# Feed-forward up products of a Strassen-type kernel: a new order of the seven products, with sums formed in PSUM from ScalarE's copies

## The chip, the cores and the metric

The kernel runs on one core of a Trainium2 chip. The metric is the device time of one execution in microseconds. The kernel before has a median of 3085.41 us in three runs (3083.14 to 3085.58).

## What is computed

One layer of a hybrid diffusion backbone on 2048 latent and 128 context tokens of width 1024. The change touches the first half of the feed-forward part alone, here cut from the reference:

```python
def finish_layer(x, ao, co, gate_a, shift_f, scale_f, gate_f, ...):
    mix = jnp.concatenate([ao, co], axis=-1) @ w_out
    x = x + gate_a * rms_norm(mix, g_attn_post)
    u = rms_norm(x, g_ffn_pre) * (1.0 + scale_f) + shift_f
    gu = u @ w_ffn_in                                  # 1024 -> 2 * 2816
    h = jax.nn.silu(gu[..., :D_FF]) * gu[..., D_FF:]
    return x + gate_f * rms_norm(h @ w_ffn_out, g_ffn_post)
```

## The kernel before

The program is written in the order of the work; a scheduling layer then sets the order of instructions on each engine, with a timeline of its own, so neighbours in the code need not be neighbours on an engine. Each engine runs its own list strictly in order. All DMAs are issued from one queue, SP's.

The product u @ w_ffn_in is a 2 by 2 block product by a Strassen-Winograd scheme: seven products in place of eight. The 17 token tiles are cut in three chunks (c = 0, 1, 2) of 320, 384 and 384 columns, and the 2816 hidden columns in 22 slices (f); `up_unit` (L948 on) does one (c, f), so there are 66 units. A unit is seven products of 12 matmuls each (L956, L957, L959), since every operand is split in a high and a low part (`split`, L81 on ScalarE makes the high part, L82 on VectorE the low one) and three of the four part products are taken, over four slices of the contraction.

Weights of a unit: `wi_raw` loads two 512 KB tiles, `wi_ops` (L908 on) makes the seven weight operands from the four blocks a11, a12, a21, a22 with four sums s1 to s4 by GpSimd (L918, tile st, 2 buffers) and seven splits. The operands lie in three buffers of two operands and one of two buffers for the seventh, so a unit's first operands can be written when the unit before is done with its own first two.

Token operands: seven as well. `build_tile` (L829 on) loads a tile of 128 tokens, GpSimd scales its rows (L835), TensorE transposes it in eight pieces (L841), four into one PSUM bank, and each piece is modulated on its way out of PSUM (L842: times one scalar per partition, plus another). `build_pair` takes two such tiles, forms differences (tile td, L859, GpSimd) and hands seven operands to `out`. For chunk 0 this happens ahead of the units, between the matmuls of the output projection (tile psx), and the operands stay on the chip. For chunks 1 and 2 it happens inside the units of the chunk before, one pair after each of f = 2, 8 and 14 (`build_spilled`): each operand is split into tile hl, which has one buffer, and stored (u2d<-hl); the next operand's split waits until that store has landed.

PSUM: eight banks, as four tags a, b, c, d with two buffers each. A unit takes one of each (ba, bb, bc_, bd), the transposes of `build_spilled` take banks of tag d. In a unit before, ScalarE copies the first product out to SBUF (p1, L965), VectorE adds it to the second (L968) and to the fifth (L973), adds the third and subtracts the fourth (L975, L976), and adds the seventh (L983); products 5, 6 and 7 are added by TensorE onto what stands in banks bb, ba and bc_. ScalarE takes the silu of both gates (L979, L984), VectorE and GpSimd multiply (L981, L986). The results (hid) go to memory for the down products (tile psy), which follow all 66 units.

## Time and profile before

| | us |
|---|---|
| median of three runs | 3085.41 |
| the profiled execution, its own time | 3085.89 |
| its span, first to last instruction | 3084.1 |
| first matmul of the up products | 1551.07 |
| first matmul of chunk 1 / chunk 2 / last unit | 1874.41 / 2234.20 / 2540.08 |
| last matmul of the up products | about 2557.3 |
| busy in the span: TensorE / VectorE / ScalarE / GpSimd | 2914.8 / 2082.6 / 1348.7 / 1242.9 |

The profiled execution is 1.8 us longer than its span and 0.5 us longer than the median. A busy TensorE is not TensorE at its peak, since matmuls overlap and their ends are modelled: what a stage loses is read from the spacing of matmul starts. The list of waits names, for each instruction that stood idle before it ran, what released it.

### The profile page before, as it was taken

What the parts mean: (1) busy time and instruction counts of PE and PEld (TensorE: products, weight loads), DVE (VectorE), ACT (ScalarE), POOL (GpSimd) and SP (SyncE); (2) the same over time, 40 slices, a digit from 0 to 9 for tenths busy, and PEclk for the clock granted to TensorE, in tenths of its full rate; (3) what the DMA queues carried; (4) which work ended last, traced back from release to release, by engine and by line L of the source; (5) the groups of instructions that cost most, each with busy time, mean ns of one, the idle gap of its engine ahead of it and who ended that gap; (6) DMA issues with size and microseconds to landing.
All of it is one profiled execution on the core that took longest, in us unless ns stands there. A gap on an engine that the chain in (4) does not pass through costs nothing.

```text
span 3084.1 us, 47310 instructions
## 1 busy us (share of the span) xinstructions
PE 2914.8 (95%) x16921; PEld 2653.6 (86%) x16921; DVE 2082.6 (68%) x4158; ACT 1348.7 (44%) x2383; POOL 1242.9 (40%) x1114
## 2 busy tenths in 40 slices
PE   4899989999999999999999989999999999999998
PEld 3778879998999999988888888999999998788886
DVE  7999568787788887764477775776665554554443
ACT  3323236666565665653344433333333333444432
POOL 7313135554545544532256654554544540111110
PEclk8999999999999999999999999999999999999999
DMA  7777564453454444457645465444632325766663
GB/s 249 249 246 246 171 196 123 136 183 113 136 166 127 139 150 132 119 164 223 183 136 156 150 195 193 145 148 134 238 137 97 102 99 193 239 223 219 219 216 120
DMA packets 351180, 525.25 MB, mean 170 GB/s; under 512 B 33089, under 2 KB 264673, under 8 KB 349153
## 3 DMA queue, kind: packets, MB, share of 16 engines
q1 hardware_dynamic: 350944, 522.23, 52.8%
q8 instruction: 133, 2.18, 0.3%
q14 instruction: 103, 0.84, 0.1%
HBM read 393.79 MB, written 128.34 MB: 169 GB/s over the span
## 4 chain that ended last, share of the span: by engine, by line
PE 65%; DVE 12%; DMA 9%; issue 7%; POOL 4%; ACT 2%; SPq 1%; POOLq 0%; DVEq 0%; ACTq 0%
PE psg L956 6%; PE s L502 6%; PE psg L959 6%; PE psg L957 6%; PE psy L1087 4%; PE psy L1086 4%; PE psy L1085 4%; PE t L546 3%; DVE wi L82 3%; DMA raw<-in_w_fi 2%; PE pq L239 2%; POOL st L918 2%; PE psx L725 2%; PE psx L726 2%; PE psx L724 2%
## 5 line engine op out<-in xcount | busy, mean ns | idle before, releaser
L956 PE MATMUL psg<-u,wi 128*128 128x384 f32 (+1 forms) x1848 | 615.6, 334 | 47.2 <-ACT wi L81 21.1
L957 PE MATMUL psg<-u,wi 128*128 128x384 f32 (+1 forms) x1848 | 606.1, 328 | 0.0
L959 PE MATMUL psg<-u,wi 128*128 128x384 f32 (+1 forms) x1848 | 590.6, 330 | 6.0 <-DVE wi L82 6.0
L505 DVE TENSOR_SCALAR_CACHE_REDUCE e<-s 128x436 f32<-128x436 f32 (+2 forms) x648 | 373.8, 600 | 90.0 <-PE s L502 73.4
L956 PEld LDWEIGHTS psg<-u,wi 128*128 128x128 f32 x1848 | 350.0, 189 | 65.7 <-ACT wi L81 29.6
L502 PE MATMUL s<-km,qt 128*128 128x436 f32 (+1 forms) x1280 | 345.7, 374 | 12.1 <-DVE e L505 9.1
L959 PEld LDWEIGHTS psg<-u,wi 128*128 128x128 f32 x1848 | 347.7, 190 | 10.8 <-DVE wi L82 10.3
L957 PEld LDWEIGHTS psg<-u,wi 128*128 128x128 f32 x1848 | 350.4, 190 | 0.1
L82 DVE TENSOR_TENSOR wo<-rawo,wo 128x1024 fp32r<-128x1024 f32 x132 | 167.0, 1265 | 248.4 <-ACT wo L81 243.7
L82 DVE TENSOR_TENSOR wi<-st,wi 128x512 fp32r<-128x512 f32 x264 | 235.2, 895 | 127.6 <-ACT wi L81 126.1
L510 ACT ACTIVATE e<-e,nm 128x2176 f32<-128x2176 f32 (+1 forms) x136 | 274.0, 2015 | 78.4 <-DVE nm L509 77.7
L81 ACT CAST wi<-st 128x512 fp32r<-128x512 f32 x264 | 163.0, 620 | 323.8 <-POOL st L918 166.2
L1087 PE MATMUL psy<-wo,hhl 128*128 128x512 f32 x748 | 285.8, 391 | 1.8 <-DVE hhl L82 1.8
L1086 PE MATMUL psy<-wo,hhl 128*128 128x512 f32 x748 | 286.3, 390 | 0.9 <-DVE wo L82 0.9
L1085 PE MATMUL psy<-wo,hhl 128*128 128x512 f32 x748 | 285.8, 390 | 0.0
L81 ACT CAST wo<-rawo 128x1024 fp32r<-128x1024 f32 x132 | 139.2, 1054 | 296.2 <-PE psy L1087 286.4
L502 PEld LDWEIGHTS s<-km,qt 128*128 128x128 f32 x1280 | 211.0, 192 | 24.4 <-DVE e L505 15.9
L82 DVE TENSOR_TENSOR atl<-t,ath 128x512 fp32r<-128x512 f32 (+2 forms) x292 | 187.1, 650 | 34.7 <-ACT ath L81 33.9
L81 ACT CAST ath<-t 128x512 fp32r<-128x512 f32 (+2 forms) x292 | 157.2, 554 | 116.2 <-PE t L546 107.6
L918 POOL TENSOR_TENSOR st<-raw,st 128x512 f32<-128x512 f32 x66 | 103.0, 1561 | 231.1 <-DVE wi L82 231.1
L1058 POOL TENSOR_TENSOR rr<-rr,mhalf 128x1 f32<-128x1 f32 x17 | 13.1, 779 | 450.4 <-DVE rr L1057 450.4
L82 DVE TENSOR_TENSOR wi<-raw,wi 128x512 fp32r<-128x512 f32 x198 | 176.6, 892 | 15.7 <-ACT wi L81 15.7
(264 smaller groups left out, 7092.6 us busy)
## 6 DMA issues: line engine op xcount, KB each, us to landing
raw<-in_w_fi SPq DMA_DIRECT2D x132, 512.0 KB, 4.1
rawo<-in_w_fo SPq DMA_DIRECT2D x132, 512.0 KB, 3.4
fu<-ud SPq DMA_DIRECT2D x256, 256.0 KB, 4.7
raw<-in_w_ada SPq DMA_DIRECT2D x48, 512.0 KB, 5.3
u2d<-hl SPq DMA_DIRECT2D x42, 512.0 KB, 3.7
u<-u2d SPq DMA_DIRECT2D x14, 1536.0 KB, 9.4
hr<-hid SPq DMA_DIRECT2D x110, 192.0 KB, 3.5
hid<-hid SPq DMA_DIRECT2D x88, 192.0 KB, 2.1
```

The lines of the kernel that those rows point to most:

```text
L81: S.copy(h, src)
L82: (eng or V).tensor_tensor(l, src, h.bitcast(F32), op=ALU.subtract)
L502: mm = T.matmul(ps[:, :n], qt[:, s, m, t * P:(t + 1) * P], km[m][:, k0:k0 + n], start=(s == 0), stop=(s == 1))
L505: V.tensor_scalar(et[:, k0:k0 + n], ps[:, :n], SCALE, None, op0=ALU.mult, op1=ALU.max, accum_out=mx[:, ci:ci + 1])
L510: S.activation(et[:, :nk], et[:, :nk], AF.Exp, bias=nm, scale=1.0, accum_out=sm[:, t, m:m + 1])
L918: G.tensor_tensor(t, x, y, op=op)
L956: T.matmul(ps[:, :n], h[:, ks], u[:, 0, kt, :n], start=start and kt == 0, stop=False, skip_group_check=not start)
L957: T.matmul(ps[:, :n], h[:, ks], u[:, 1, kt, :n], start=False, stop=False, skip_group_check=not start)
L959: T.matmul(ps[:, :n], l[:, ks], u[:, 0, kt, :n], start=False, stop=stop and kt == 3, skip_group_check=not start)
L1085: T.matmul(banks[i][:, b, :], hh, woh_[:, bs], start=(f == 0), stop=False)
L1086: T.matmul(banks[i][:, b, :], hh, wol_[:, bs], start=False, stop=False)
L1087: T.matmul(banks[i][:, b, :], hl, woh_[:, bs], start=False, stop=(f == NF - 1))
```

## The change

It has four parts.

1. **Another order and other sums.** Product 1 goes to bank ba and ScalarE copies it, PSUM to PSUM, into bb; product 2 goes to bc_ and ScalarE copies it to SBUF (p5); product 3 is added by TensorE onto bb, and ScalarE copies bb into bd; products 4, 5, 6 and 7 are added onto ba, bb, bd and bb again. VectorE adds p5 to bb (c22, ahead of product 7) and to bd (u2), and multiplies the silu of ba with bb itself. Per unit VectorE has three operations outside the splits in place of six, ScalarE three copies in place of one.
2. **The weight operands** are made in the order in which the new products use them: a11, s1, s2, a12, s3, s4, a22 (before a11, s2, s1, a22, s3, a12, s4). The token operands are numbered to match.
3. **Modulation** of the built tiles is ScalarE's (Identity with scale and bias from memory) in place of VectorE's: 40 pieces ahead of the units and 96 inside them.
4. **Banks.** The transposes of `build_spilled` take tag c (before d). In the first two units one matmul of 512 columns is added on each of bb and bd, so that later matmuls there add onto what ScalarE wrote.

```diff
--- before.py
+++ after.py
@@ -839,8 +840,8 @@
             for a in range(4):
                 kt = 4 * kk + a
                 T.transpose(up[:, a, :], row[:, kt * P:(kt + 1) * P], ident)
-                V.tensor_scalar(ur[:, kt, :], up[:, a, :], modc[:, 2, c, kt:kt + 1], modc[:, 3, c, kt:kt + 1],
-                                op0=ALU.mult, op1=ALU.add)
+                S.activation(ur[:, kt, :], up[:, a, :], AF.Identity, scale=modc[:, 2, c, kt:kt + 1],
+                             bias=modc[:, 3, c, kt:kt + 1])
         return ur
 
     def build_pair(pair, bank, out):
@@ -860,13 +861,13 @@
             return t
 
         out(0, w, b11)
-        out(5, w, b21)
-        out(6, w, b22)
+        out(3, w, b21)
+        out(5, w, b22)
         t = diff(b12, b11)
-        out(2, w, t)
+        out(1, w, t)
         t2_ = diff(b22, t)
-        out(1, w, t2_)
-        out(3, w, diff(t2_, b21))
+        out(2, w, t2_)
+        out(6, w, diff(b21, t2_))
         out(4, w, diff(b22, b12))
 
     def pst_bank():
@@ -928,15 +929,15 @@
                 dst.append((q[:, 0], q[:, 1]))
         split(*dst[0], a11)
         s1 = total(a21, a22, ALU.add)
+        split(*dst[1], s1)
         s2 = total(s1, a11, ALU.subtract)
-        split(*dst[1], s2)
-        split(*dst[2], s1)
-        split(*dst[3], a22)
-        s4 = total(a12, s2, ALU.subtract)
+        split(*dst[2], s2)
+        split(*dst[3], a12)
         s3 = total(a11, a21, ALU.subtract)
         split(*dst[4], s3)
-        split(*dst[5], a12)
-        split(*dst[6], s4)
+        s4 = total(a12, s2, ALU.subtract)
+        split(*dst[5], s4)
+        split(*dst[6], a22)
         return dst
 
     def t(tag, n, bufs=1):
@@ -948,42 +949,43 @@
     def up_unit(c, f, ws, us):
         n = widths[c]
 
-        def product(ps, i, start, stop):
+        def product(ps, i, start):
             h, l = ws[i]
             u = us[i]
             for kt in range(4):
                 ks = slice(kt * P, (kt + 1) * P)
-                T.matmul(ps[:, :n], h[:, ks], u[:, 0, kt, :n], start=start and kt == 0, stop=False, skip_group_check=not start)
-                T.matmul(ps[:, :n], h[:, ks], u[:, 1, kt, :n], start=False, stop=False,
-                         skip_group_check=not start)
-                T.matmul(ps[:, :n], l[:, ks], u[:, 0, kt, :n], start=False, stop=stop and kt == 3,
-                         skip_group_check=not start)
+                T.matmul(ps, h[:, ks], u[:, 0, kt, :n], start=start and kt == 0, stop=False, skip_group_check=not start)
+                T.matmul(ps, h[:, ks], u[:, 1, kt, :n], start=False, stop=False, skip_group_check=not start)
+                T.matmul(ps, l[:, ks], u[:, 0, kt, :n], start=False, stop=kt == 3, skip_group_check=not start)
 
         ba, bb, bc_, bd = (bank(x) for x in "abcd")
-        product(ba, 0, True, True)
-        p1_ = t("p1", n)
-        S.copy(p1_, ba[:, :n])
-        product(bb, 1, True, True)
+        if c == 0 and f < 2:
+
+            for x in (bb, bd):
+                T.matmul(x, ws[0][0][:, :P], ws[0][0], start=True, stop=True)
+        ba, bb, bc_, bd = (x[:, :n] for x in (ba, bb, bc_, bd))
+        product(ba, 0, True)
+        S.copy(bb, ba)
+        product(bc_, 1, True)
+        p5 = t("p5", n)
+        S.copy(p5, bc_)
+        product(bb, 2, False)
+        S.copy(bd, bb)
+        product(ba, 3, False)
+        sg = t("sg", n)
+        S.activation(sg, ba, AF.Silu)
+        product(bb, 4, False)
+        c22 = t("c22", n)
+        V.tensor_tensor(c22, bb, p5, op=ALU.add)
+        product(bd, 5, False)
         u2_ = t("u2", n)
-        V.tensor_tensor(u2_, bb[:, :n], p1_, op=ALU.add)
-        product(bc_, 2, True, True)
-        product(bd, 3, True, True)
-        product(bb, 4, False, True)
-        u3 = t("u3", n)
-        V.tensor_tensor(u3, bb[:, :n], p1_, op=ALU.add)
-        c22 = t("c22", n)
-        V.tensor_tensor(c22, bc_[:, :n], u3, op=ALU.add)
-        V.tensor_tensor(u3, u3, bd[:, :n], op=ALU.subtract)
-        product(ba, 5, False, True)
-        sg = t("sg", n)
-        S.activation(sg, ba[:, :n], AF.Silu)
-        ha = t("hid", n, 2)
-        V.tensor_tensor(ha, sg, u3, op=ALU.mult)
-        product(bc_, 6, False, True)
-        V.tensor_tensor(u2_, u2_, bc_[:, :n], op=ALU.add)
+        V.tensor_tensor(u2_, bd, p5, op=ALU.add)
         S.activation(u2_, u2_, AF.Silu)
         hb = t("hid", n, 2)
         G.tensor_tensor(hb, u2_, c22, op=ALU.mult)
+        product(bb, 6, False)
+        ha = t("hid", n, 2)
+        V.tensor_tensor(ha, sg, bb, op=ALU.mult)
         if c:
             dma(hidd[c][f][:, 0:n], ha)
             dma(hidd[c][f][:, n:2 * n], hb)
@@ -1001,7 +1003,7 @@
             split(hl[:, 0, :, :w], hl[:, 1, :, :w], src)
             dma(u2d[c, i][:, :, :, k * P:k * P + w], hl[:, :, :, :w])
 
-        build_pair(chunks[c][k], lambda: bank("d"), out)
+        build_pair(chunks[c][k], lambda: bank("c"), out)
 
     def u_load(pool_, i, c):
         u = pool_.tile([P, 2, 4, 384], F32R, tag="u", name="u2", bufs=2 if pool_ is pua else 7)
```

What this does to the order on ScalarE in the steady part, one unit of chunk 2 (wi are weight operands, st the sums, psg the PSUM banks). Before:

```order
L81 CAST wi_26337<-raw4_26226 128x512
L81 CAST wi_26337<-st_26345 128x512
L965 COPY p1_26246<-psg_26230 128x384
L81 CAST wi_26338<-st_26343 128x512
L81 CAST wi_26338<-raw4_26228 128x512
L81 CAST wi_26340<-st_26353 128x512
L984 ACTIVATE u2_26123<-u2_26123 128x384
L979 ACTIVATE sg_26315<-psg_26230 128x384
L81 CAST wi_26339<-st_26355 128x512
L81 CAST wi_26339<-raw4_26226 128x512
```

Now:

```order
L81 CAST wi_26101<-raw4_25991 128x512
L971 COPY p5_26022<-psg_25995 128x384
L81 CAST wi_26098<-raw4_25989 128x512
L81 CAST wi_26098<-st_26104 128x512
L973 COPY psg_25996<-psg_25994 128x384
L976 ACTIVATE sg_26049<-psg_25993 128x384
L81 CAST wi_26099<-st_26108 128x512
L81 CAST wi_26099<-raw4_25989 128x512
L81 CAST wi_26100<-st_26114 128x512
L968 COPY psg_26129<-psg_26128 128x384
L983 ACTIVATE u2_26077<-u2_26077 128x384
L81 CAST wi_26100<-st_26118 128x512
```

The two silus and seven casts are still there; L965's copy has become L968, L973 and L971, and L968, the copy of a unit's first product, stands between the two casts of its third weight buffer.

ScalarE again, in the first build (after f = 2 of chunk 0), at the last two operands that are stored from hl. Before:

```order
L81 CAST hl_18859<-td_18857 128x512
L81 CAST wi_19288<-st_19304 128x512
L81 CAST wi_19288<-raw4_19173 128x512
L81 CAST wi_19425<-raw4_19312 128x512
L965 COPY p1_19332<-psg_19316 128x320
L81 CAST wi_19425<-st_19433 128x512
L81 CAST wi_19426<-st_19431 128x512
L81 CAST wi_19426<-raw4_19314 128x512
L81 CAST hl_18865<-td_18863 128x512
L984 ACTIVATE u2_19207<-u2_19207 128x320
```

Now:

```order
L81 CAST hl_18857<-td_18855 128x512
L976 ACTIVATE sg_19227<-psg_19171 128x320
L81 CAST wi_19279<-st_19288 128x512
L81 CAST wi_19279<-raw4_19167 128x512
L81 CAST wi_19280<-st_19294 128x512
L81 CAST hl_18863<-td_18861 128x512
L968 COPY psg_19309<-psg_19308 128x320
L983 ACTIVATE u2_19255<-u2_19255 128x320
```

The casts into hl stand among the weight casts as before, but a PSUM copy (L968) now stands right behind one. Over all six builds, between a cast into hl of a difference (td) and the cast into hl ahead of it, ScalarE's list had 105 instructions in 24 stretches before, and has 132 now; in 9 of the 24 places a copy L968 or L973 stands among the next three instructions.

TensorE at the transposes of the second tile in that build. Before (banks psg_18802 and psg_18815 take the transposes):

```order
L959 MATMUL psg_19038<-u0_0_16972,wi_19008 128x320
L841 MATMUL psg_18802<-ident_60,row_18789 128x128
L841 MATMUL psg_18815<-ident_60,row_18811 128x128
L956 MATMUL psg_18900<-u0_4_16976,wi_18871 128x320
L957 MATMUL psg_18900<-u0_4_16976,wi_18871 128x320
L959 MATMUL psg_18900<-u0_4_16976,wi_18871 128x320
L956 MATMUL psg_18900<-u0_4_16976,wi_18871 128x320
L957 MATMUL psg_18900<-u0_4_16976,wi_18871 128x320
```

Now (banks psg_18813 and psg_18822):

```order
L957 MATMUL psg_19034<-u0_3_16975,wi_19005 128x320
L958 MATMUL psg_19034<-u0_3_16975,wi_19005 128x320
L842 MATMUL psg_18813<-ident_60,row_18809 128x128
L959 MATMUL psg_19034<-u0_3_16975,wi_19005 128x320
L957 MATMUL psg_19034<-u0_3_16975,wi_19005 128x320
L842 MATMUL psg_18822<-ident_60,row_18809 128x128
L958 MATMUL psg_19034<-u0_3_16975,wi_19005 128x320
L959 MATMUL psg_19034<-u0_3_16975,wi_19005 128x320
L842 MATMUL psg_18813<-ident_60,row_18809 128x128
L842 MATMUL psg_18822<-ident_60,row_18809 128x128
L957 MATMUL psg_19035<-u0_4_16976,wi_19006 128x320
L958 MATMUL psg_19035<-u0_4_16976,wi_19006 128x320
```

Ten matmuls or more stood between two transposes into one bank before (three times in the six builds only two); now the two banks of a tile are filled side by side, most of the rounds stand 20 or more matmuls apart, and ten rounds in the six builds stand two to five matmuls apart.

## Rows read from the trace of the kernel before

**Rows 1.** Busy time by stretch: the last stretch of the output projection with the building of chunk 0's operands, chunk 0, chunk 1, 21 units of chunk 2, the last unit. Columns: length, then busy time and instructions of TensorE, its weight loads, VectorE, ScalarE and GpSimd, granted clock, share of DMA, GB/s.

```profile
1399.00:1551.00 152.00, 152.00 (x686) 124.15 (x684) 67.33 (x115) 58.37 (x131) 34.97 (x43) 1.00 0.64 197
1551.07:1874.41 323.34, 293.64 (x1896) 281.05 (x1897) 251.54 (x359) 132.45 (x250) 192.73 (x134) 0.98 0.50 154
1874.41:2234.20 359.79, 338.01 (x1898) 328.00 (x1897) 239.33 (x358) 132.47 (x244) 181.30 (x128) 0.99 0.52 175
2234.20:2540.08 305.88, 305.88 (x1766) 305.72 (x1765) 175.78 (x273) 112.30 (x210) 151.50 (x105) 1.00 0.33 111
2540.08:2557.30 17.22, 14.94 (x85) 14.30 (x85) 10.00 (x15) 5.69 (x8) 1.00 (x1) 1.00 0.36 116
```

**Rows 2.** The timeline of TensorE in chunk 0, at two matmuls that stand eight steps apart in a dense stretch (start, length).

```profile
1859.96 0.31 PE L956 MATMUL psg<-u,wi 128*128 128x320 f32 x1
...
1861.13 0.31 PE L959 MATMUL psg<-u,wi 128*128 128x320 f32 x1
```

**Rows 3.** Waits of TensorE's weight loads in chunks 0 and 1 (1551 to 2235 us): who waited for whom, us in total, times, longest.

```profile
PEld psg L956 <- ACT wi L81: 29.4, 27, 4.0
PEld psg L956 <- DVE u L968: 11.0, 13, 2.6
PEld psg L959 <- DVE wi L82: 10.3, 16, 1.2
PEld psg L956 <- DVE c L975: 5.4, 4, 3.2
PEld psg L956 <- DVE u L976: 4.8, 6, 0.8
PEld psg L956 <- DMA u<-u2d: 3.7, 1, 3.7
PEld psg L956 <- issue: 3.4, 2, 2.1
PEld psg L956 <- ACT p L965: 1.9, 3, 0.9
PEld psg L956 <- DVE ur L842: 1.4, 3, 0.6
PEld psg L841 <- DVE ur L842: 0.7, 1, 0.7
```

**Rows 4.** The same in chunk 2 (2235 to 2558 us).

```profile
PEld psg L956 <- DVE c L975: 1.6, 1, 1.6
PEld psg L956 <- DVE u L968: 1.4, 1, 1.4
```

**Rows 5.** Busy time by stretch, columns as in Rows 1: two of the six stretches of 3.4 us in chunks 0 and 1 in which the granted clock was half.

```profile
1737.80:1741.20 3.40, 3.40 (x15) 3.40 (x14) 3.40 (x6) 1.49 (x4) 1.33 (x1) 0.50 0.55 158
2079.10:2082.50 3.40, 3.25 (x11) 3.16 (x11) 3.37 (x8) 1.68 (x4) 0.00 (x0) 0.51 0.55 160
```

**Rows 6.** VectorE's groups in the up products (busy us, mean ns of one, idle before and what ended it).

```profile
L842 DVE TENSOR_SCALAR ur<-psg,modc 128x128 f32<-128x128 f32 x96 | 36.8, 402 | 14.5 <-PE psg L841 14.4
L981 DVE TENSOR_TENSOR hid<-sg,u 128x384 f32<-128x384 f32 x44 | 32.0, 727 | 5.0 <-ACT sg L979 3.9
L975 DVE TENSOR_TENSOR c<-psg,u 128x384 f32<-128x384 f32 x44 | 24.4, 555 | 1.2
L968 DVE TENSOR_TENSOR u<-psg,p 128x384 f32<-128x384 f32 x44 | 24.4, 554 | 32.2 <-POOL hid L986 32.2
L983 DVE TENSOR_TENSOR u<-u,psg 128x384 f32<-128x384 f32 x43 | 23.6, 549 | 16.9 <-PE psg L959 16.8
L968 DVE TENSOR_TENSOR u<-psg,p 128x320 f32<-128x320 f32 x22 | 10.7, 487 | 13.8 <-POOL hid L986 13.6
```

**Rows 7.** ScalarE's groups in the whole span, columns as in Rows 6 (on<-tq, sg, p, tt and psx<-psx read PSUM, the last writes PSUM too; oc<-on and u<-u read SBUF, and oc<-on has one scale from memory).

```profile
L85 ACT ACTIVATE oc<-on,orr 128x128 fp32r<-128x128 f32 x68 | 23.8, 396 | 12.7 <-POOL orr L576 12.7
L984 ACT ACTIVATE u<-u 128x384 f32<-128x384 f32 x44 | 23.0, 522 | 23.4 <-DVE u L983 23.4
L979 ACT ACTIVATE sg<-psg 128x384 f32<-128x384 f32 x44 | 21.5, 488 | 27.9 <-PE psg L959 27.9
L965 ACT COPY p<-psg 128x384 f32<-128x384 f32 x44 | 20.8, 473 | 4.5 <-DVE u L973 4.1
L728 ACT ACTIVATE psx<-psx 128x512 f32<-128x512 f32 x34 | 20.2, 594 | 0.0
L727 ACT COPY tt<-psx 128x512 f32<-128x512 f32 x34 | 19.9, 584 | 34.8 <-PE psx L726 26.1 <-DMA x2d<-tt 8.4
L965 ACT COPY p<-psg 128x320 f32<-128x320 f32 x22 | 9.2, 420 | 2.7 <-DVE u L973 2.5
L570 ACT COPY on<-tq 128x128 f32<-128x128 f32 x4 | 1.0, 260 | 0.9 <-PE tq L568 0.9
```

**Rows 8.** Waits of ScalarE in the up products (columns as in Rows 3).

```profile
ACT hl L81 <- DMA u2d<-hl: 50.8, 17, 5.5
ACT hl L81 <- DVE ur L842: 15.0, 15, 1.8
```

**Rows 9.** The chain that ended last, in the first build (1596 to 1660 us): its shares by line.

```profile
by line: DVE wi L82 31.9%; issue 14.3%; DVE hl L82 11.6%; DMA raw<-in_w_fi 6.1%; DMA u2d<-hl 5.9%; DVE ur L842 4.8%; POOL hid L986 4.8%; POOL st L918 3.0%; DVE c L975 2.6%; DVE hid L981 2.4%; DMA hid<-hid 2.2%; DVE u L973 1.9%; PE psg L956 
```

**Rows 10.** Waits of ScalarE from 1399 to 1556 us, ahead of the units (columns as in Rows 3).

```profile
ACT xr L738 <- DVE tt L735: 31.9, 8, 5.0
```

**Rows 11.** The DMA issues of the stores of built operands: count, size, median us from issue to landing.

```profile
u2d<-hl SPq DMA_DIRECT2D x42, 512.0 KB, 3.7
```

## The prediction, made before the changed kernel ran

> **What bounds the kernel now.** First the busy time by stretch [rows 1], since the change lies between 1551 and 2557 us, with a part ahead of it. Ahead of it TensorE is busy for all of the 152 us. In 21 units of chunk 2 it is so too: 305.88 us for 21 times 84 matmuls are 0.1734 us each. In chunk 1, with the same size of matmul, 22 units took 359.79 us where 1848 x 0.1734 = 320.4 would do: 39.4 us are lost. In chunk 0 the timeline gives the pace of the smaller matmul, 1.17 us for eight steps or 0.146 [rows 2]; 1848 of them are 269.8 us, and the stretch took 323.34: 53.5 us lost. The last unit loses 17.22 - 14.56 = 2.7. So 95.6 us of TensorE's time is all that a change here can win, beside work that it takes away, and it takes none away from TensorE.
>
> Next, who TensorE waits for [rows 3]; three classes. (a) VectorE has not yet read a PSUM bank that a product or a transpose is to write: L968 11.0, L975 5.4, L976 4.8, L842 1.4 + 0.7, together 23.3. (b) A weight operand is late: its cast on ScalarE 29.4, its low part on VectorE 10.3, together 39.7. (c) The rest: 3.7 + 3.4 + 1.9 = 9.0. That is 72.0 of 92.9; of the remaining 20.9, six stretches of 3.4 us with a granted clock of 0.5 (1.2 GHz) [rows 5] cost about 6 x 1.7 = 10.2; they follow or hold waits of TensorE. The rest is transposes and waits too short to be listed.
>
> Why are (a) and (b) late? VectorE was busy 251.54 of 323.34 us in chunk 0, 78%, and 67% in chunk 1 [rows 1], and in the first build the chain that ended last runs mostly through it [rows 9]. ScalarE is far less busy, 41% and 37%, but strictly in order: in all it stood 50.8 us at the cast into hl, which waits for the store of the operand before [rows 8, 11], and weight casts stood behind it.
>
> **The change, part by part.** VectorE loses three additions per unit. The six operations of a 384 unit were five of 0.55 us (L968, L975, L983 and two like them) and L981's 0.727, 3.49 in all [rows 6]; left are two like L975 and a product that reads one operand from PSUM, as L983 does, 1.66: 1.83 less. For a 320 unit three like L968, 3 x 0.487 = 1.46 less. With 48 pieces of modulation per chunk at 0.402 = 19.3, VectorE's load in chunk 0 falls by 22 x 1.46 + 19.3 = 51 us (20%) and in chunk 1 by 22 x 1.83 + 19.3 = 60 (25%). In chunk 2 this lies beside a TensorE that never waits: worth nothing there.
>
> ScalarE gains two copies per unit, 0.420 or 0.473 us each, 18 to 21 us per chunk (that they write PSUM adds little: 594 ns against 584 at 512 columns) [rows 7], and the modulation. The trace has no such piece on ScalarE. Below it is bounded by a plain copy of 128 x 128 from PSUM, 0.260. Above: a copy grows (473 - 260) / 256 = 0.83 ns per column, so a function from PSUM without operands from memory takes 488 - 256 x 0.83 = 275 ns at 128; from SBUF 522 - 213 = 309, where the one with a scale from memory takes 396 [rows 7], so each such operand adds 87, and scale and bias make 275 + 174 = 449. I take 0.45, since the change uses both; that is not less than VectorE's 0.402, so the move pays by relief of VectorE, not by speed. The Trainium skill (ScalarE: Activation LUTs, Rules for kernel authors) even advises VectorE, not ScalarE, for multiply and add, and its section What ACT_TABLE_LOAD costs gives 186 ns + 0.833 ns per element + 93 ns for each operand from memory, by which a piece would take about 479 ns, an estimate (the row of 396 agrees with its 386 for one such operand); by that price ScalarE would be busy 96 x 0.03 = 3 us longer and the sum below 0.3 us smaller. With 0.45, ScalarE's load in chunk 0 becomes 132.45 + 18.5 + 48 x 0.45 = 173 us, still 57% of 300.
>
> On TensorE, class (a): the waits for L968, L976 and L842 go with their instructions: 11.0 + 4.8 + 2.1 = 17.9. The wait for the read of c22 stays (L975's 5.4); I halve it, since the change relieves the engine that is late: 2.7 more. In their place TensorE waits for ScalarE's copies. In the steady order the first product's end and the third product's start are more than 20 matmuls apart, 3 us or more against a copy of 0.47; the nearest row is L965, a copy that TensorE already waits for, 1.9 us in 44 units [rows 3]. Three copies at that rate are 5.7, so 3.8 more. Upper bound: they cost what L968 and L976 cost, 15.8; lower bound zero. The ten rounds of transposes that stand two to five matmuls apart wait for ScalarE: two pieces of 0.45 less some 0.4 of matmuls, with a transpose's 0.27 ahead; I take 0.6 each, 6 us (0 to 10). Class (a) gives 20.6 - 3.8 - 6 = 10.8, bounds -5 and 20.6.
>
> Class (b): ScalarE's list has 132 instructions in place of 105 between the casts into hl of differences. At some 0.5 us that is 13.5 us of work in place of standing: 50.8 becomes 37, or 27% less [rows 8]. Of 29.4 I take 27%, 7.9. For VectorE's 10.3 I take 40%, 4.1, twice its relief, as a queue shrinks faster than its load. Together 12.0, bounds 0 (the store's landing sets the pace all the same) and two thirds, 26.
>
> The half clock: a third of 10.2 goes with the longest waits, 3.4 (bounds -3, 8). The last unit waited for L968 and L975 [rows 4]; L968 is gone and a copy has a whole product as cover: 1.7 (0 to 2.7). The added matmuls of 512 columns: four, under 1 us: -0.9.
>
> What costs nothing. The 40 modulations ahead of the units: TensorE is full there [rows 1], and between two transposes of one bank stand some 24 matmuls of 0.23 us, 5.6 us, more than ScalarE's longest standstill at L738, 5.0 [rows 10]; if that cover fails, it is a part of a microsecond for each of 20 rounds, inside the range. The other order of weight operands: the second needs one GpSimd sum in place of two, the last block is a22, loaded with the first. The product ha is now formed after product 7, so its store, and what SP has queued behind it (weight loads and stores of hl), is issued later; two units of weights are loaded ahead, which hides it, and if not, an hl store that comes 1 us later costs ScalarE as much, again in (b)'s lower bound. Chunk 2: every copy has 20 matmuls or more ahead of its use: zero.
>
> Sum: 10.8 + 12.0 + 3.4 + 1.7 - 0.9 = 27.0. From the profiled execution's 3085.9, 3058.9; against the median, 0.5 lower, 3058.4: **3058**. The bounds alone give gains of -9 (3094) and 56 (3029).
>
> **The rivals.**
> *ScalarE's queue becomes the gate* (slower). In nine of the 24 places a PSUM copy stands within three instructions behind a cast into hl, and now TensorE itself waits for that copy. For: ScalarE stood there 3.0 us on average and up to 5.5 [rows 8], and the modulation brings the casts into hl from ur forward (the 15.0 us that they waited for L842 go). Against: the cover of 3 us or more. It decides once the standstill outlasts the matmuls between the copied product and its first use. Without cover nine places cost 9 x 3.0 = 27 to 9 x 5.5 = 50 us, and the 7.9 of the casts is not won; the other 19 stay. So a net 8 to 31 lost: about 3100.
> *The chain is the same* (no change). If the stores of hl, one buffer and about 5.4 us each (cast, low part, landing 3.7 [rows 11]), set the pace of the build units whatever VectorE does, the waits only change their names and the last unit alone wins: 3083.
> *VectorE's load was the root of it all* (faster by more). Then (a) keeps only some 3 us, two thirds of (b) and most of the half clock go: 20 + 26 + 7 + 2 = 55: 3030.
> *It doesn't do what it says*: the scheduling layer could undo the order; its lists show the moves made, so I give it no chance of its own.
>
> **How the numbers follow.** Forecast (a gain of 10 to 45 us) 0.52, more than that 0.16, same 0.14, ScalarE as the gate 0.18. The measurement tells 0.2%, 6.2 us, from no change. Part of "the same" may still win over 6 us, and part of the gate may end within it: faster 0.69, same 0.14, slower 0.17. The range runs from the bound at 3029 to just past the lower bound at 3094, since the gate's worst and the best case each have some 0.1 beyond: 3028 to 3097.
>
> **What would show it.** Right: chunks 0 and 1 together 22 to 27 us shorter, chunk 2 at the same 14.56 us per unit; VectorE's busy time in the units about 150 us less; in TensorE's waits no VectorE line but c22 and low parts above 2 us, ScalarE's copies below 8; pieces of modulation near 0.45 us; ScalarE's stand at hl near 37. Wrong: waits of TensorE for L968 or L973 above 20 us, or a stand at hl above 50 (the gate); the same loss in chunks 0 and 1 with other names (the chain); chunk 2 slower per unit, which nothing above allows.

## The result and the profile after

The changed kernel has a median of 3062.41 us in four runs (3057.11 to 3067.98), the kernel before 3084.27 on the same chip (3080.99 to 3085.58): a ratio of 0.9931, 95% interval 0.9918 to 0.9943; the medians differ by 22 us. The profiled execution took 3067.98 us, with a span of 3066.2; it was the longest of the four, and the span is 17.9 us shorter than before.

Busy time by stretch of the changed kernel, columns as in [rows 1]: the last stretch of the output projection, chunk 0, chunk 1, 21 units of chunk 2, the last unit.

```profile
1399.00:1548.00 149.00, 149.00 (x674) 121.91 (x673) 53.46 (x74) 71.19 (x168) 34.97 (x43) 1.00 0.64 198
1548.28:1862.13 313.85, 290.41 (x1900) 281.55 (x1899) 220.65 (x248) 163.16 (x342) 185.90 (x132) 0.98 0.52 159
1862.13:2217.93 355.80, 336.62 (x1898) 328.11 (x1897) 206.93 (x244) 164.59 (x335) 179.31 (x128) 0.99 0.54 174
2217.93:2523.69 305.76, 305.76 (x1765) 305.76 (x1765) 167.79 (x210) 129.50 (x252) 144.03 (x105) 1.00 0.34 114
2523.69:2538.08 14.39, 14.39 (x84) 14.39 (x84) 6.59 (x9) 6.87 (x11) 2.37 (x3) 1.00 0.45 146
```

The first up product starts 2.8 us earlier, chunk 0 is 9.5 us shorter, chunk 1 4.0, the last unit 2.8; chunk 2 is the same. VectorE is busy 31 and 32 us less in chunks 0 and 1, not 51 and 60, and only 8 less in chunk 2: 602 us in the up products in place of 677, half of the relief that was forecast.

What TensorE's weight loads waited for in the up products, against [rows 3]; the columns are the same.

```profile
PEld psg L957 <- ACT wi L81: 15.5, 15, 3.5
PEld psg L959 <- DVE wi L82: 13.5, 13, 1.9
PEld psg L957 <- ACT psg L968: 12.3, 12, 2.0
PEld psg L842 <- ACT ur L843: 5.1, 8, 1.9
PEld psg L957 <- DMA u<-u2d: 4.2, 1, 4.2
PEld psg L957 <- DVE c L979: 3.9, 4, 1.3
PEld psg L965 <- ACT wi L81: 1.7, 2, 1.4
```

Of VectorE's reads of PSUM only c22 (L979) is left. In their place stands the first copy, L968. Late casts fell from 29.4 to 17.2, and late low parts rose from 10.3 to 13.5.

ScalarE's stand at the cast into hl, against [rows 8], and its groups in the up products, against [rows 7] (busy us, mean ns, idle before and what ended it).

```profile
ACT hl L81 <- DMA u2d<-hl: 75.7, 29, 7.0
```

```profile
L843 ACT ACTIVATE ur<-psg,modc 128x128 f32<-128x128 f32 x96 | 41.0, 457 | 4.8 <-PE psg L842 4.5
L968 ACT COPY psg<-psg 128x384 f32<-128x384 f32 x44 | 20.8, 473 | 2.9 <-PE psg L959 2.9
L81 ACT CAST hl<-td 128x512 fp32r<-128x512 f32 x24 | 14.9, 621 | 58.4 <-DMA u2d<-hl 56.5 <-DVE c L979 1.8
L81 ACT CAST hl<-ur 128x512 fp32r<-128x512 f32 x18 | 11.1, 618 | 19.2 <-DMA u2d<-hl 19.1
```

A piece of modulation took 457 ns, a copy into PSUM 473, as one into SBUF did. The stand at hl grew from 50.8 us to 75.7. Before, the casts of the modulated tiles (hl<-ur) waited for VectorE's modulation [rows 8]; now they too arrive before the store of the operand ahead has landed.

The low parts on VectorE, groups of L82 in the up products; the kernel before, whose rows of these groups were not shown, then the changed one.

```profile
L82 DVE TENSOR_TENSOR wi<-st,wi 128x512 fp32r<-128x512 f32 x264 | 235.2, 895 | 127.6 <-ACT wi L81 126.1
L82 DVE TENSOR_TENSOR wi<-raw,wi 128x512 fp32r<-128x512 f32 x198 | 176.6, 892 | 15.7 <-ACT wi L81 15.7
```

```profile
L82 DVE TENSOR_TENSOR wi<-st,wi 128x512 fp32r<-128x512 f32 x264 | 246.1, 935 | 160.8 <-ACT wi L81 157.0
L82 DVE TENSOR_TENSOR wi<-raw,wi 128x512 fp32r<-128x512 f32 x198 | 233.0, 1193 | 35.5 <-ACT wi L81 30.7 <-DMA raw<-in_w_fi 4.6
```

The same 462 instructions take 67 us more. Where it comes from shows in a piece of chunk 2 of the changed kernel in order of time (start, length, instruction), VectorE and then GpSimd (lines cut):

```profile
2342.04 0.68 DVE L82 TENSOR_TENSOR wi<-st,wi 128x512 fp32r<-128x512 f32 x1
2344.62 0.69 DVE L82 TENSOR_TENSOR wi<-raw,wi 128x512 fp32r<-128x512 f32 x1
2353.67 3.02 DVE L82 TENSOR_TENSOR wi<-raw,wi 128x512 fp32r<-128x512 f32 x2
```

```profile
2350.48 1.28 POOL L919 TENSOR_TENSOR st<-raw,st 128x512 f32<-128x512 f32 x1 [6.33 <-DVE wi L82]
2352.69 1.75 POOL L919 TENSOR_TENSOR st<-raw 128x512 f32<-128x512 f32 x1
2354.52 1.62 POOL L919 TENSOR_TENSOR st<-st,raw 128x512 f32<-128x512 f32 x1
```

A low part takes 0.68 to 0.69 us while GpSimd is idle, and two take 3.02 while GpSimd forms sums. The second of the two ends at 2356.69, 0.55 us after the end of the second sum. That is so throughout: of the low parts of the changed kernel, 242 start while a GpSimd operation on two tensors is running, and each of them ends 0.54 to 0.56 us after the end of that operation. So such a low part stands until GpSimd is done. The Trainium skill (SBUF — State Buffer, Who interferes with whom) says that a VectorE instruction with two inputs in SBUF contends with a GpSimd instruction that reads SBUF; the timeline agrees.

Counted over the up products, 298 of the 462 low parts overlap a GpSimd operation on two tensors for a tenth of their time or more, where 236 did before, and the time of overlap is 280 us in place of 202; the other 164 have a mean of 684 ns. The new order puts two low parts of raw blocks (a22 and the next unit's a11) beside the first two sums: in chunk 2 these take 1.34 and 1.76 us on average, where no low part of a raw block had a mean above 0.74 before.

### The profile page after: what moved, and what is told of

The parts are those of the page before. It is cut to its first block, busy times and chain, and to the rows that moved or that the text cites. A ratio compares the mean times of both kernels' runs of the same rounds, so it can differ in the third digit from the quotient of the medians.

```text
span 3066.2 us, 47162 instructions
## 1 busy us (share of the span) xinstructions
PE 2909.8 (95%) x16925; PEld 2653.8 (87%) x16925; DVE 1994.7 (65%) x3824; ACT 1444.4 (47%) x2651; POOL 1230.1 (40%) x1114
## 5 line engine op out<-in xcount | busy, mean ns | idle before, releaser
L959 PEld LDWEIGHTS psg<-u,wi 128*128 128x128 f32 x1848 | 348.1, 189 | 13.9 <-DVE wi L82 13.5
L82 DVE TENSOR_TENSOR wi<-st,wi 128x512 fp32r<-128x512 f32 x264 | 246.1, 935 | 160.8 <-ACT wi L81 157.0
L82 DVE TENSOR_TENSOR wo<-rawo,wo 128x1024 fp32r<-128x1024 f32 x132 | 167.0, 1265 | 252.3 <-ACT wo L81 252.3
L82 DVE TENSOR_TENSOR wi<-raw,wi 128x512 fp32r<-128x512 f32 x198 | 233.0, 1193 | 35.5 <-ACT wi L81 30.7
L82 DVE TENSOR_TENSOR atl<-t,ath 128x512 fp32r<-128x512 f32 (+2 forms) x292 | 187.1, 649 | 36.4 <-ACT ath L81 35.7
L919 POOL TENSOR_TENSOR st<-raw,st 128x512 f32<-128x512 f32 x66 | 87.3, 1322 | 254.4 <-DVE wi L82 254.4
```

The lines of the kernel that those rows point to most:

```text
L82: (eng or V).tensor_tensor(l, src, h.bitcast(F32), op=ALU.subtract)
L919: G.tensor_tensor(t, x, y, op=op)
L959: T.matmul(ps, l[:, ks], u[:, 0, kt, :n], start=False, stop=kt == 3, skip_group_check=not start)
```

## The experiments

Three questions were open: whether VectorE's relief makes the gain, what the modulation on ScalarE is worth, and what the collisions of low parts with GpSimd's sums cost. All ratios are to the kernel before on the same chip. "Up products" is the time from the first matmul of the units to the end of the last, in the profiled execution; it leaves out the start, which varied between 1545.5 and 1554.2 us. The other columns are sums of the lists of waits, us; a late cast or low part is one of a weight operand that TensorE's weight loads waited for.

| kernel | median | ratio, 95% interval | up products | late casts | late low parts | ScalarE's stand at hl |
|---|---|---|---|---|---|---|
| before | 3084.27 | 1 | 1006.6 | 29.4 | 10.3 | 50.8 |
| changed | 3062.41 | 0.9931 [0.9918, 0.9943] | 990.1 | 17.2 | 13.5 | 75.7 |
| after_again | 3060.82 | 0.9928 [0.9915, 0.9940] | 987.0 | 16.9 | 14.1 | 70.2 |
| e1 | 3053.25 | 0.9903 [0.9888, 0.9918] | 974.9 | 9.0 | 11.7 | 51.6 |
| e10 | 3052.38 | 0.9897 [0.9882, 0.9912] | 979.7 | 7.2 | 10.8 | 53.8 |
| e2 | 3075.95 | 0.9973 [0.9962, 0.9984] | 999.5 | 21.6 | 10.5 | 24.3 |
| e3 | 3058.51 | 0.9914 [0.9901, 0.9928] | 979.8 | 8.1 | 10.0 | 14.6 |
| e4 | 3084.41 | 0.9999 [0.9988, 1.0011] | 1005.5 | 12.5 | 22.6 | 14.5 |
| e5 | 3064.85 | 0.9934 [0.9920, 0.9947] | 983.3 | 4.0 | 11.4 | 14.8 |
| e6 | 3059.93 | 0.9925 [0.9909, 0.9940] | 983.8 | 10.3 | 12.4 | 52.9 |
| e7 | 3086.35 | 1.0008 [0.9999, 1.0017] | 1008.5 | 5.4 | 7.4 | 76.8 |
| e8 | 3029.83 | 0.9822 [0.9806, 0.9838] | 952.4 | 8.7 | none listed | 60.2 |
| e9 | 3065.80 | 0.9943 [0.9929, 0.9957] | 989.0 | 8.8 | 7.7 | 62.6 |
| e11 | 3030.32 | 0.9829 [0.9814, 0.9844] | 957.3 | 7.0 | 8.0 | 59.0 |

### The changed kernel again

> The changed kernel as it is, on the chip of the runs below, so that they are compared with it and not with an earlier call. Both theories: ratio to the kernel before 0.992 to 0.995, 3057 to 3068 us.

3060.82 us, a ratio of 0.9928: the first comparison holds on a second chip, where the medians differ by 24 us.

### The modulation: back on VectorE (e1, and again as e10), and alone on ScalarE in the kernel before (e2)

e1 and e10, against the changed kernel:

```diff
-                S.activation(ur[:, kt, :], up[:, a, :], AF.Identity, scale=modc[:, 2, c, kt:kt + 1],
-                             bias=modc[:, 3, c, kt:kt + 1])
+                V.tensor_scalar(ur[:, kt, :], up[:, a, :], modc[:, 2, c, kt:kt + 1], modc[:, 3, c, kt:kt + 1],
+                                op0=ALU.mult, op1=ALU.add)
```

e2 makes the opposite edit in the kernel before.

> The changed kernel with the modulation of the built tiles back on VectorE (136 pieces). Theory 1 (the gain is relief of VectorE): VectorE is busy 39 us longer in the units, about a third of what the change took from it there, so a third of the 22 us goes: 3067 to 3070. Theory 2 (ScalarE's queue, with its stand at the cast into hl, is what still costs): ScalarE has 41 us less to do and its copies come sooner: 3055 to 3059, waits of TensorE for the copy L968 well below 12 us.

> The kernel before with the modulation alone moved to ScalarE; the seven products and their sums as before. Theory 1: VectorE loses 39 us of load in chunks 0 and 1, so 6 to 9 us faster than before: 3075 to 3078. Theory 2: ScalarE's queue gets 41 us longer and weight casts come later, no gain or up to 6 us slower: 3084 to 3090.

> e1_mod_on_vector once more, since the changed kernel with modulation half or not at all on ScalarE gave 3053, 3060 and 3065 in three forms. If the 9 us are real: ratio to the kernel before 0.988 to 0.992, 3050 to 3058, and from the first to the last matmul of the up products 972 to 978 us (974.6 in the first run, 990 and 987 in two profiles of the changed kernel). If they were the chip's or the day's: 0.992 to 0.995 and 984 us or more.

In the kernel before, the modulation on ScalarE gains 8 us, as theory 1 of e2 has it. In the changed kernel it costs 9: without it the time is 3053.25, and 3052.38 the second time (its up products, 979.7, are 2 us above what was expected). That is the way of theory 2 of e1, and below its 3055; but the waits for L968 are 10.9, not well below 12. So the rest of the change is worth 31 us: the products and sums with the order of the weight operands and the banks, which no run takes apart. The waits of TensorE in e1:

```profile
PEld psg L959 <- DVE wi L82: 11.7, 11, 1.9
PEld psg L957 <- ACT psg L968: 10.9, 10, 2.1
PEld psg L842 <- DVE ur L843: 8.0, 13, 1.2
PEld psg L957 <- ACT wi L81: 7.0, 8, 1.7
```

Late casts are 9.0 us in all in place of 17.2, and ScalarE stands at hl 51.6 us in place of 75.7. The waits of the transposes hardly tell the two apart: 8.0 here, 5.6 there. So by these lists the price of the pieces on ScalarE is paid in late casts, behind a longer stand at hl. Followed back to the last standstill of ScalarE ahead of each wait, over half a microsecond and at most 6 us before, the stand at hl is behind 9.3 of the 17.2 us of late casts in the changed kernel and behind 2.3 of 9.0 in e1. That the stand must grow with them is not so: in e2 the same edit brought it from 50.8 down to 24.3, and late casts from 29.4 to 21.6. The two kernels differ in what holds ScalarE up ahead of hl, and the runs don't settle why the stand moves the other way.

### Half of the pieces on ScalarE (e6)

```diff
+                if kk:
+                    V.tensor_scalar(ur[:, kt, :], up[:, a, :], modc[:, 2, c, kt:kt + 1], modc[:, 3, c, kt:kt + 1],
+                                    op0=ALU.mult, op1=ALU.add)
+                else:
+                    S.activation(ur[:, kt, :], up[:, a, :], AF.Identity, scale=modc[:, 2, c, kt:kt + 1], ...
```

> The changed kernel with four of the eight pieces of each tile modulated by ScalarE and four by VectorE. If the price of ScalarE's pieces is proportional to their number: midway, 3056 to 3059, ScalarE's stand at hl about 64 us (between 51.6 and 75.7). If it is a matter of one late piece that holds the chain from tile to tile (the second four are the ones that GpSimd's differences wait for): as with all on VectorE, 3052 to 3055, stand near 52.

3059.93 us. That is near the changed kernel's, and its interval also takes in the middle; the stand at hl, 52.9, is e1's. Neither expectation is met as a whole, and the run decides nothing about the price of a piece.

### A second buffer of hl: in the changed kernel (e3), in the kernel before (e4), and with modulation on VectorE (e5)

```diff
-            hl = bld.tile([P, 2, 4, P], F32R, tag="hl", name="hl", bufs=1)
+            hl = bld.tile([P, 2, 4, P], F32R, tag="hl", name="hl", bufs=2)
```

> The changed kernel with two buffers for hl in place of one, so that a cast into hl need not wait for the landing of the store just before. Theory 2: ScalarE's stand of 75.7 us at hl falls below 20 us, and with it TensorE's waits for the copy L968, the casts and part of the half clock: 20 to 30 us faster than the changed kernel, about 3037. Theory 1: operands are late because of VectorE and GpSimd all the same: at most 8 us faster, 3054 or more.

> The kernel before with two buffers for hl. Theory 2: its stand of 50.8 us at hl goes and TensorE's wait for casts (29.4) falls by half: 15 to 25 us faster, about 3064. Theory 1: VectorE at 78% stays the root: at most 8 us faster, 3076 or more.

> The changed kernel with the modulation back on VectorE and a second buffer of hl. Each alone gave 3053.25 and 3058.51 beside 3062.4. Theory 1 (the modulation on ScalarE costs because the piece lengthens the wait of ScalarE's list at hl, which one buffer makes): with two buffers there is nothing more for it to cost, so the two gains are the same one and the time is 3051 to 3055. Theory 2 (the time of the pieces on ScalarE costs in itself, the second buffer is another gain): the gains add, 9 + 4 us, 3046 to 3050. ScalarE's stand at hl below 20 us in both.

The stand at hl goes to some 15 us in all three. That is worth nothing in the kernel before: late casts fall by 16.9 us and late low parts rise by 12.3, which points to VectorE's queue behind ScalarE's. In the changed kernel it is worth some 4 us, its interval overlapping the changed kernel's. Theory 1 is met in both kernels. In the changed one TensorE waits 9.1 us less for casts then, but 11.9 us for c22 in place of 3.9. On top of e1 it costs 12 us by the medians and 10 by the ratios, against both expectations. VectorE in e5, in order of time:

```profile
1602.82 1.78 DVE L82 TENSOR_TENSOR hl<-ur,hl 128x512 fp32r<-128x512 f32 x1
1604.52 0.40 DVE L843 TENSOR_SCALAR ur<-psg,modc 128x128 f32<-128x128 f32 x1
1604.84 0.67 DVE L82 TENSOR_TENSOR wi<-st,wi 128x512 fp32r<-128x512 f32 x1
1605.44 0.40 DVE L843 TENSOR_SCALAR ur<-psg,modc 128x128 f32<-128x128 f32 x1
1605.76 1.72 DVE L82 TENSOR_TENSOR hl<-ur,hl 128x512 fp32r<-128x512 f32 x1
```

The low parts of hl, each 1.7 us, now come without the pause that one buffer made, and c22, for which TensorE waits 10.4 us in five places here, stands behind them in the three longest of these waits. This goes with a longer chunk 0 (317.3 us against 309.5 in e1), and is not shown to be all of the loss: the profiled execution of e5 took 3058.11 us and the other four 3.5 to 7.6 us more, which no trace shows.

### The copies on VectorE (e7)

As e1, and in addition:

```diff
-        S.copy(bb, ba)
+        V.tensor_copy(bb, ba)
...
-        S.copy(bd, bb)
+        V.tensor_copy(bd, bb)
```

> The changed kernel with modulation and the two copies from PSUM to PSUM on VectorE, so that ScalarE has one copy per unit, as before the change, and VectorE five operations outside the splits. Theory 1 (relief of VectorE is what the new order pays by): the 20 us of copies that VectorE takes back in each chunk cost 10 us or more, 3063 to 3072, and TensorE waits for the copies on VectorE as it waited for L968 of before, 11 us or more. Theory 2 (TensorE's waits are set by ScalarE's standstills at hl, 10.9 us for the copy L968 with modulation on VectorE): those waits go, 3045 to 3051.

3086.35 us: 33 more than e1, and none of the gain is left. VectorE, then TensorE, in chunk 1 of e7:

```profile
2144.48 0.69 DVE L82 TENSOR_TENSOR hl<-ur,hl 128x512 fp32r<-128x512 f32 x1 [1.15 <-ACT hl L81]
2145.09 0.56 DVE L968 COPY psg<-psg 128x384 f32<-128x384 f32 x1
```

```profile
2145.79 0.66 PE L957 MATMUL psg<-u,wi 128*128 128x384 f32 x1 [3.93 <-DVE psg L968]
```

The copy stands in VectorE's list behind a low part of hl, that waits for ScalarE's cast, and the cast for the store. The list of waits of e7 has "issue: 31.6, 10, 4.6" for these loads; by the records, 12 matmuls for which TensorE had stood over 1 us, 36.6 us together, started 0.15 us after the end of a copy L968. Ahead of five of these copies (18.9 us) VectorE had stood idle for a cast into hl; the other seven came behind low parts without a pause, of 0.7 to 1.8 us each. Theory 1 is right in its direction, but its bound of 3072 is passed by 14 us. So it is shown that the gain hangs on having these copies off VectorE's list. That VectorE's load as such is what counts is not shown: e11, below, keeps VectorE busy for longer than the kernel before, and is 54 us faster.

### GpSimd's sums left out (e8), and formed but unread (e9)

e8, against the changed kernel; the weight operands are made of the blocks themselves, so this is another computation. e9 does the same and keeps the four calls of `total`.

```diff
-        s1 = total(a21, a22, ALU.add)
-        split(*dst[1], s1)
-        s2 = total(s1, a11, ALU.subtract)
-        split(*dst[2], s2)
+        split(*dst[1], a21)
+        split(*dst[2], a22)
         split(*dst[3], a12)
-        s3 = total(a11, a21, ALU.subtract)
-        split(*dst[4], s3)
-        s4 = total(a12, s2, ALU.subtract)
-        split(*dst[5], s4)
+        split(*dst[4], a11)
+        split(*dst[5], a12)
```

> The changed kernel without the four sums of the weight blocks that GpSimd forms in each unit: the operands are made of the blocks themselves (a11, a21, a22, a12, a11, a12, a22), so the output is not the layer's. Low parts of weight operands on VectorE then run beside no such sum: both theories expect their mean near the 0.69 us that they take alone, in place of 1.19 (from a block) and 0.94 (from a sum), some 150 us less of VectorE's time. Theory 1 (the collisions took the relief of VectorE that the forecast counted on): 10 us or more faster than e9_sums_unread. Theory 2 (VectorE has slack enough in most units, the collisions only fill it): within 4 us of e9_sums_unread.

> As e8_no_sums, the operands are made of the blocks, but GpSimd forms the four sums all the same and nothing reads them, so that its load is there and nobody waits for it. Both theories: means of the low parts above 0.9 us again. Theory 1: 10 us or more slower than e8_no_sums. Theory 2: within 4 us of it. Beside the changed kernel it shows what waiting for the sums costs: 88 us of ScalarE's standing goes, at most the 14 us that TensorE waited for late casts, so 3046 to 3062.

The low parts of 21 units of chunk 2, e8 and then e9:

```profile
L82 DVE TENSOR_TENSOR wi<-raw,wi 128x512 fp32r<-128x512 f32 x147 | 96.0, 689 | 69.3 <-ACT wi L81 67.3
```

```profile
L82 DVE TENSOR_TENSOR wi<-raw,wi 128x512 fp32r<-128x512 f32 x147 | 144.8, 1020 | 58.2 <-ACT wi L81 56.0
```

In e9 no other engine waits for a sum, and yet it takes 36 us longer than e8. The price of the sums is thus GpSimd's presence, and theory 1 holds: 256 of the 462 low parts of e9 overlap GpSimd, 298 in the changed kernel, 59 in e8, and the low parts take 496 us in e9 and 336 in e8. A longer list on GpSimd would be another reason, but TensorE's waits that go back to it are small: 1.9 us for a scaled row, 2.0 for a c22 that stood for GpSimd's product. The 36 us are the price of nearly all collisions, not of those that the new order added; and they hold what follows the waits, such as 20.5 us at a granted clock of half in e9, 6.8 in e8. And e9 is no faster than the changed kernel, where ScalarE stood 88.3 us for sums: late casts fell from 17.2 to 8.8 us, but TensorE waited 22.6 us for c22 in place of 3.9, and in the longest of these waits low parts of 1.3 to 1.8 us stood ahead of it in VectorE's list.

### The sums on VectorE (e11)

As e1, and in addition:

```diff
-            G.tensor_tensor(t, x, y, op=op)
+            V.tensor_tensor(t, x, y, op=op)
```

> The changed kernel with modulation on VectorE (as e1_mod_on_vector, 3053.25 and 3052.38) and the four sums of the weight blocks on VectorE too, in place of GpSimd. Theory 1 (the collision of VectorE's low parts with GpSimd's sums costs more than the sums): four sums at the 0.69 us that such an operation takes alone are 2.8 us per unit more for VectorE, and the low parts get back about what e9_sums_unread and e8_no_sums differ by in chunk 2, (177.97 - 130.89) / 21 = 2.2 us per unit, so VectorE's load in chunk 0 stays within 10 us of e1's 241.5, and the casts no longer wait for sums of 1.5 us each: 3035 to 3050. Theory 2 (a sum on VectorE stands in the queue behind low parts and its cast waits longer than for GpSimd): 3056 to 3070, and ScalarE's waits for st above the 115 us of e1.

3030.32 us: 22 less than e1, 54 less than the kernel before, and below either bound that was expected. Chunk 0, chunk 1 and 21 units of chunk 2 of e11, then groups of VectorE in chunk 2:

```profile
1549.92:1843.57 293.65, 283.98 (x1900) 276.95 (x1898) 242.28 (x389) 144.91 (x295) 53.32 (x42) 1.00 0.56 171
1843.57:2186.77 343.20, 332.89 (x1898) 327.82 (x1897) 240.66 (x379) 146.47 (x286) 57.56 (x40) 0.99 0.55 180
2186.77:2492.53 305.76, 305.76 (x1766) 305.76 (x1765) 197.94 (x294) 128.37 (x252) 29.25 (x21) 1.00 0.34 114
```

```profile
L82 DVE TENSOR_TENSOR wi<-st,wi 128x512 fp32r<-128x512 f32 x84 | 57.6, 687 | 38.6 <-ACT wi L81 35.6
L919 DVE TENSOR_TENSOR st<-raw 128x512 f32<-128x512 f32 x21 | 28.4, 1353 | 0.7
L919 DVE TENSOR_TENSOR st<-raw,raw 128x512 f32<-128x512 f32 x21 | 14.5, 692 | 0.7
```

VectorE has four operations more per unit than in e1 and is busy 242 us in chunk 0, as in e1 (241.5): there the low parts give back what the sums take. In chunk 1 it is busy 241 us against 223, in chunk 2 198 against 168, and in all of the up products 689 us, against 639 in e1 and 677 in the kernel before. So e11 is the faster by 22 and by 54 us with VectorE busy for longer, not for less. TensorE waits for VectorE's low parts 8.0 us in place of 11.7 and for its pieces 4.9 in place of 8.0. 59.6 us of ScalarE's standing in the list of e11 are for sums, and 151 have no named releaser, so how long it waits for sums there stays open. Whether e11 gains by the shorter low parts or by GpSimd's free list was not taken apart.

## Why the prediction was right

The forecast was 3058 and its sum 27.0 us; the span shrank by 17.9, the medians differ by 22 and 24 us on the two chips. The sign and the stage were right. The reason, relief of VectorE, holds in so far as the gain goes when the copies return to VectorE (e7); it fails as a matter of VectorE's busy time, of which half as much went as forecast, and which in e11 is above that of the kernel before. The move of the modulation, counted as 19.3 us of relief in each chunk, costs 9 us in the changed kernel (e1). So that the number came near is in part luck: terms that were too large and terms that were too small stand side by side.

Of the signs that the prediction set, these came: chunk 2 at 14.56 us per unit, pieces near 0.45 us, and of VectorE only c22 and low parts above 2 us. These did not: chunks 0 and 1 are 13.5 us shorter, not 22 to 27; VectorE is busy 75 us less, not 150; the copies cost 12.7, not below 8; and the stand at hl, 75.7, is above the 50 that was to show ScalarE's gate. The terms of the sum came out like this:

- **VectorE's reads of PSUM.** 23.3 us of waits became 3.9 (c22): 19.4 gone, 20.6 forecast. But not all of it was VectorE's load. In the kernel before, VectorE stood idle ahead of L968 until GpSimd's product L986 had read u2, which has one buffer (its waits in the up products, and one of them in order of time):

```profile
DVE u L968 <- POOL hid L986: 45.8, 45, 3.3
```

```profile
1625.51 0.49 DVE L968 TENSOR_TENSOR u<-psg,p 128x320 f32<-128x320 f32 x1 [3.31 <-POOL hid L986]
```

  Six of TensorE's 13 waits for L968, 6.0 of the 11.0 us, followed such a standstill, and before L976 (4.8) VectorE had stood for TensorE's own product. The new order has no addition in these places. The prices of the copies on ScalarE, 0.42 and 0.473 us, and of the piece, 0.457 against 0.45, were right.
- **The copies.** The step "three copies at that rate are 5.7" was mis-sized by more than a factor of two: 12.7 (L968 12.3, L973 0.4). The rate was taken from a copy that stood elsewhere in ScalarE's list. The rival of ScalarE's queue named the mechanism, a copy behind a cast into hl; it cost 11 us more than L965 did, not 27 to 50. Behind 8.5 of L968's 12.3 us ScalarE's last standstill was the one at hl.
- **The transposes.** 6 forecast, 5.6 measured. So this class gave 19.4 - 10.8 - 5.6 = 3.0, where 10.8 were forecast.
- **The late casts.** 12.2 us gone, 7.9 forecast, but not by the step given. "50.8 becomes 37" failed: the stand at hl rose to 75.7, and about half of the growth from e1's 51.6 is at the casts of the modulated tiles (19.1 us behind a store, 6.8 in e1). The forecast let added work fill the stand; that is what e2 shows, and e7 beside e1 the other way round (two copies fewer per unit on ScalarE, a stand of 76.8 in place of 51.6), but not the changed kernel. Followed back as in e1, the late casts behind the stand at hl went from 14.7 to 9.3 us, those behind a weight buffer that TensorE still read from 5.2 to none, and those behind a sum from 5.5 to 5.0. Taking the pieces off ScalarE (e1) or giving hl a second buffer (e3) halves the late casts that are left.
- **The low parts.** 4.1 less forecast, 3.2 more measured. The step that failed is "VectorE's load falls by 51 and 60 us": the 51 and 60 of removed instructions are right, but 20 and 28 us come back, most of it (17 and 26) in low parts of weight operands, which in the new order stand for GpSimd more often and longer. What these added collisions cost in time was not measured by themselves.
- **The half clock.** A third less was forecast; it hardly shrank. Before, six stretches of 3.4 us at a granted clock of 0.5 (1.2 GHz) [rows 5], 20.5 us; now four of them and one twice as long, 20.5 again, and 17.1 in after_again. Two of them; the second began while TensorE stood 3.9 us for chunk 1's token operands, the first after waits of 0.6 and 1.0 us for a cast and a low part:

```profile
2072.90:2076.30 3.40, 3.37 (x11) 3.38 (x12) 2.86 (x3) 0.59 (x2) 1.59 (x1) 0.50 0.07 13
1875.00:1881.80 6.80, 5.32 (x17) 5.32 (x18) 0.00 (x0) 0.46 (x1) 0.00 (x0) 0.50 1.01 428
```

- **The last unit.** 2.8 gained, 1.7 forecast; chunk 2 unchanged, as forecast. Nothing was forecast for the start, which came 2.8 us earlier; as it varies by 8.7 us between these kernels, it is not put down to the change. These terms make 14.8 of the 16.5 us by which the up products shrank; the rest, with the added matmuls and the waits too short to be listed, was not taken apart.

Of the rivals, "the chain is the same" is out: the gain is clear of the noise on two chips, and a second buffer of hl alone gains nothing (e4). "VectorE's load was the root of it all" gave 3030 as its time, and e11 reaches that, but by another road: with more instructions on VectorE and more busy time, not less. In e8 and e11, the two fastest, VectorE's low parts hardly meet GpSimd's operations any more (59 and 45 of the 462), and e9 beside e8 shows what it costs when they do.

Open is why the price of the modulation sits mostly in chunk 1 (lost time of TensorE there, the length of the chunk less the 320.4 us of a dense one: 35.4 and 33.3 us in the two profiles of the changed kernel, 24.5 and 24.6 in e1 and e10), and why half of the pieces cost about as much as all of them.

## What to carry to other kernels

Cost a relief of an engine by the time that its remaining instructions will take in the new order: a mean from the trace before holds their collisions, and a new order can bring more of them. An operation is cheapest on the engine where it is least in the way: moving sums to VectorE, the busiest engine beside TensorE, paid here, where its own low parts took 1.24 us on average beside GpSimd and 0.68 without. Busy time alone doesn't tell what an engine costs another; look at what stands in its list ahead of the instruction that is waited for. Where an engine stands at a one-buffer store, what another engine waits for is better not queued behind it; a second buffer gained little here, as another queue held the same work up.

## What the hardware showed that was not expected

- A VectorE difference of two 128x512 tiles took 0.68 to 0.69 us with GpSimd idle, and up to 1.79 with a GpSimd operation on two tensors beside it (a mean of 1.24 over the 298 of the changed kernel). One that started while such an operation was running always ended 0.54 to 0.56 us after it (242 of them): the two don't share the time, the low part stands until GpSimd is done. GpSimd's sums took 1.26 to 1.30 us in the 64 cases without a VectorE operation on two SBUF tensors beside them, and 1.56 on average, at most 1.85, with one.
- The same holds for the sums that e11 forms on VectorE. The sum of the two halves of one loaded tile (st<-raw, a21 and a22) has a mean of 1353 ns in chunk 2, where sums over two tiles take 692, but that is its place in the order, beside GpSimd's product. With GpSimd idle it takes 0.69 us too (23 of the 66). VectorE, VectorE, and GpSimd:

```profile
1845.06 0.69 DVE L919 TENSOR_TENSOR st<-raw 128x512 f32<-128x512 f32 x1
2349.10 1.39 DVE L919 TENSOR_TENSOR st<-raw 128x512 f32<-128x512 f32 x1
```

```profile
2348.52 1.41 POOL L985 TENSOR_TENSOR hid<-u,c 128x384 f32<-128x384 f32 x1 [13.14 <-ACT u L983]
```

- A copy from PSUM to PSUM on ScalarE took what a copy from PSUM to SBUF took, 473 ns at 384 columns.
- One and the same kernel, e1 and e10, took 309.52 and 314.22 us for chunk 0, at mean granted clocks of 0.98 and 0.96:

```profile
1554.16:1863.68 309.52, 289.24 (x1900) 281.65 (x1898) 241.49 (x296) 147.44 (x294) 191.10 (x132) 0.98 0.53 162
```

```profile
1545.50:1859.72 314.22, 294.25 (x1899) 286.79 (x1898) 242.14 (x296) 147.34 (x294) 191.29 (x132) 0.96 0.51 160
```
